# Splitting queries, keys and values where they are produced, loading heads one ahead, spacing the head norm, and moving attention traffic to GpSimd's DMA queue

## The chip, the cores and the metric

One core of a Trainium2 chip runs the whole program. The metric is device time in microseconds (us) of one execution; three executions of the kernel before gave a median of 3043.97 us.

## The reference: what is computed

One layer of a hybrid encoder, for a batch "s" of 1024 tokens and a batch "p" of 512 tokens, model width 2048, all in fp32:

```python
def mixer_layer(x, ...):
    h = rms_norm(x, norm_g) @ w_in
    qa, ka, va, ga, qb, kb, vb, gb = split(h)        # 5376 columns of features, 1280 of values
    oa = window_gqa(qa, ka, va, sink, rel_bias)      # A: 16 heads of 64, 4 key heads, keys within 128 tokens
    ob = diff_attention(qb, kb, vb, lam, ...)        # B: 8 heads, all keys
    mixed = concatenate([silu(ga) * oa, silu(gb) * ob])
    return x + mixed @ w_out                         # then rms_norm(., final_g)

def diff_attention(q, k, v, lam, ...):               # per head, block of 128 queries
    s = einsum(q, k) * scale + bias                  # two score maps, c = 0, 1
    p = softmax(s)
    pd = p[0] - lam * p[1]
    o = pd @ v
    return rms_norm(o, subln_g) * (1 - lam_init)     # over the head's 128 columns
```

## The kernel before: tiling, stages and order

Every fp32 product is made of three float32r products: an operand is split into hi (a cast on ACT) and lo = operand - hi (a subtraction on DVE), and hi·hi, lo·hi and hi·lo are summed in PSUM. Projections (L254 `project`, L291 `in_v`) take 16 slices of 128 features; the three matmuls of a slice are L263, L264, L266 (512 columns) or L301, L303, L305 (256 columns, for values). The weights' split stands just ahead of their use: `weights` (L242) loads a tile "wr", casts "wh" on ACT (L249) and subtracts "wl" on DVE (L251).

Stages. First `in_v_all` for s (values). Then `in_fm_all` for s (42 feature tiles of queries, keys, gates) beside attention A of s. Then a main line (values and features of p, the output projection of s in two chunks, that of p) beside a side line (attention B of s, A of p, B of p). `drive` (L654) interleaves the two: each step of the side line asks for a GAP of main's work (1.05 us a step in B of s, 1.3 in B of p, 2.1 and 1.7 in A). The order on each engine is fixed when the program is built, and every engine takes its instructions in that order; all transfers stand in one queue, SP's.

Features go to DRAM (`fm_s`, `fm_p`, from `in_fm`), values to `v_s`, `v_p` (`in_v`, L314, L315), and attention loads them back unsplit. Attention A (L369): `load_head` loads the keys twice (partitions 0-63 and 64-127), splits them (L366, L376), and `load_q` (L391, L392) loads four pieces for every block of 128 queries and splits them (L393, L394). Attention B (L492): `load_head` (L497) loads strip, keys and values and splits them on ACT (L366, L511) and DVE (L505, L512) when the head begins; `load_q` (L516) does so every four blocks (L521). For a block and each of the two maps, `scores` (L524) makes s (L535, L536), takes the minimum of -(s + bias) on DVE (L538), the exponential on ACT (L542), and after the second map 1/z (L546, L547), p1 scaled on ACT (L548) and p0·z0 - p1·z1 on DVE (L549). `turn` (L551) transposes the block before (L558, into the PSUM tile "tp", one buffer in s, two in p) and splits it into "ph" on ACT (L560) and "pl" on DVE (L561). `values` (L563) multiplies with the values (L572 to L574).

When a head's values are done, `normalise` (L580) is emitted six steps later, in one go: squares, ssq (L588), 1/rms "rc" by a square root on ACT (L183, a table load before and after it) and a reciprocal on DVE (L184); rc is stored to DRAM as single elements (L591, `rstd_s`, `rstd_p`), loaded back along rows on every partition as "r" (L595), the gate is loaded (L597), and DVE multiplies gate·output (L598) and ·r (L599); the product goes to `mix` (L600), from which `load_mix` brings it into the output projection.

Of the kernel before, what the change touches and what calls it, by code (L numbers as in the profile page):

```python
# [9 lines left out]
F32 = mybir.dt.float32  # L10
# [23 lines left out]
WR = [3]  # L34
# [11 lines left out]
def kernel(  # L46
# [23 lines left out]
    dma = nc.sync.dma_start  # L70

# [7 lines left out]
    ones_r = const.tile([P, P], F32R, name="ones_r")  # L79
    V.tensor_copy(ones_r, ones)  # L80
# [8 lines left out]
    lamv = const.tile([P, 2], F32, name="lamv")  # L89
    lsum = const.tile([P, 2], F32, name="lsum")  # L90

    def constants():
# [7 lines left out]
        nc.gpsimd.memset(lamv, 1.0)  # L100
# [11 lines left out]
        V.tensor_tensor(out=lamv[:, 1:2], in0=lsum[:, 0:1], in1=lsum[:, 1:2], op=ALU.subtract)  # L112
        V.tensor_scalar(out=lamv[:, 1:2], in0=lamv[:, 1:2], scalar1=LAM_INIT, scalar2=None, op0=ALU.add)
# [39 lines left out]
    def make_batch(nm, xt, yt, ntok, normed):  # L153
# [4 lines left out]
        b.fm = [dram.tile([P, ntok], F32, name=f"fm_{nm}{c}") for c in range(N_FM)]  # L158
        b.v = [dram.tile([ntok, 256], F32, name=f"v_{nm}{g}") for g in range(5)]
        b.rstd = [dram.tile([1, ntok], F32, name=f"rstd_{nm}{h}") for h in range(HB)]  # L160
# [25 lines left out]
    def rstd_cols(acc, psp):  # L186
        """1/rms of each token from its partial sums of squares, a column per 128 tokens."""
# [7 lines left out]
    def rstd_rows(rc, psp, pool=None, **kw):  # L195
        """The same along rows, on every partition: in PSUM, or copied to a tile of the pool."""
# [31 lines left out]
    def load_mix(b, c, pool):  # L228
        """Yields after each feature tile that it has brought in and split."""
        ch = new_chunk()  # L230
        yield ch
        for k in range(KT):
            hi = pool.tile([P, TC], F32R, name="hi")
            lo = pool.tile([P, TC], F32R, name="lo")
            dma(out=raw(lo), in_=b.mix[c][k])
# [6 lines left out]
    def weights(src, wp, before=None):  # L242
        a, c = src.shape[1], src.shape[2]
        wr = wp.tile([P, a, c], F32, name="wr", bufs=WR[0])
        dma(out=wr, in_=src)
        if before:
            before()
        wh = wp.tile([P, a, c], F32R, name="wh")
        S.copy(out=wh, in_=wr)  # L249
        wl = wp.tile([P, a, c], F32R, name="wl")  # L250
        V.tensor_tensor(out=wl, in0=wr, in1=raw(wh), op=ALU.subtract)  # L251
        return wh, wl

    def project(chs, w, psp, wp, along=iter(()), ahead=iter(())):  # L254
        ps = [psp.tile([P, 512], F32, name="pp") for _ in chs]
        for part in range(4):
            for _ in range(4):
                next(ahead, None)
            wh, wl = weights(w[:, 4 * part:4 * part + 4, :], wp)
# [12 lines left out]
    def in_fm(b, chs, c, psp, wp):  # L272
        ps = yield from project(chs, w_fm[c], psp, wp)
        gate = c >= C_GA
        f = 0.125 if c < C_KB or C_QA <= c < C_KA else 1.0
        for n, ch in enumerate(chs):
            o = ev.tile([P, TC], F32, name="o", bufs=2)
            h = ps[n]
            if not b.normed:
                V.scalar_tensor_tensor(out=o, in0=h, scalar=f, in1=b.rb[n], op0=ALU.mult, op1=ALU.mult)  # L280
                h = o
            elif not gate:
                S.activation(out=o, in_=h, func=AF.Copy, scale=f)
            if gate:
                th = ev.tile([P, TC], F32, name="sq", bufs=2)
                S.activation(out=th, in_=h, func=AF.Tanh, scale=0.5)
                V.scalar_tensor_tensor(out=o, in0=th, scalar=1.0, in1=h, op0=ALU.add, op1=ALU.mult)
            dma(out=b.fm[c][:, n * TC:(n + 1) * TC], in_=o)
        done.add((b.nm, "fm", c))

    def in_v(b, chs, g, psp, wp, before=None):  # L291
        ps = [[psp.tile([P, 2, 256], F32, name="pp") for _ in range(2)] for _ in chs]
        for part in range(8):
            wh, wl = weights(w_v[g][:, 2 * part:2 * part + 2, :], wp, before and (lambda: before(g, part)))
# [15 lines left out]
        for n, ch in enumerate(chs):  # L310
            for t in range(4):
                o = ev.tile([P, 256], F32, name="ov", bufs=2)
# [8 lines left out]

    def in_fm_all(b, chs, psp, wp):
        order = []
        for pr in range(2):
            order += [C_KA + pr] + [C_QA + 4 * pr + j for j in range(4)] + [C_GA + 4 * pr + j for j in range(4)]
        for h in range(HB):
            order += [C_KB + h, C_QB + h, C_GB + h]
        for c in order:
            yield from in_fm(b, chs, c, psp, wp)

    def out_proj(b, c, mix, psp, wp, yp, before):
        """Returns the steps left for when the next products are under way: norm and store."""
# [3 lines left out]
        for d in range(KT):  # L336
            xr = yp.tile([P, TC], F32, name="xr", bufs=2)
            dma(out=xr, in_=b.xt[d * P:(d + 1) * P, c * TC:(c + 1) * TC])
            ps = yield from project([ch], w_o[d], psp, wp, before, mix)
# [4 lines left out]
        def finish(spread):  # L344
# [3 lines left out]
            for d in range(KT):  # L348
                yield
                V.scalar_tensor_tensor(out=y[d], in0=y[d], scalar=fg[:, d:d + 1], in1=r, op0=ALU.mult, op1=ALU.mult)  # L350
                dma(out=b.yt[d * P:(d + 1) * P, c * TC:(c + 1) * TC], in_=y[d])
# [8 lines left out]
    def load_qk(at, tagname, src, n, bufs=2):  # L360
        """src [64, n] rows in DRAM -> raw copy on partitions 0-63 and 64-127, and its high part."""
        lo = at.tile([P, n], F32R, name=f"{tagname}_lo", bufs=bufs)
        dma(out=raw(lo)[0:DH], in_=src)
        dma(out=raw(lo)[DH:P], in_=src)
        hi = at.tile([P, n], F32R, name=f"{tagname}_hi", bufs=bufs)
        S.copy(out=hi, in_=raw(lo))  # L366
        return hi, lo

    def attention_a(b, at, gap, pss, pst, pso, psp):  # L369
        n, nb = b.n, b.nb  # L370

        def load_head(kv):
            lo_rows = slice(DH, P) if kv % 2 == 0 else slice(0, DH)
            rows = slice(0, DH) if kv % 2 == 0 else slice(DH, P)
            k_hi, k_lo = load_qk(at, "k", b.fm[C_KA + kv // 2][(kv % 2) * DH:(kv % 2 + 1) * DH, :], n, 1)
            V.tensor_tensor(out=k_lo, in0=raw(k_lo), in1=raw(k_hi), op=ALU.subtract)  # L376
            vv = at.tile([P, nb, P], F32R, name="vv")
# [460 lines left out]
```

## Time and profile before

| | us |
|---|---|
| median of 3 runs | 3043.97 (3041.66 to 3049.67) |
| profiled execution: span from first to last instruction | 3051.6 |
| TensorE busy in it | 2897.0 (95%) |
| DVE, ACT busy | 1635.5, 1336.9 |

The profile is of one more execution. What lay around its span is not listed, so its own time is at least the span, 7.6 us above the median. "Busy" for TensorE (PE) counts a matmul from its start to its modelled end, and at half clock a matmul is busy longer. PEclk is the granted clock as a share of 2.4 GHz.

### The profile page before, as it was taken

What the parts mean: (1) busy time and instruction counts of PE and PEld (TensorE: products, weight loads), DVE (VectorE), ACT (ScalarE), POOL (GpSimd) and SP (SyncE); (2) the same over time, 40 slices, a digit from 0 to 9 for tenths busy, and PEclk for the clock granted to TensorE, in tenths of its full rate; (3) what the DMA queues carried; (4) which work ended last, traced back from release to release, by engine and by line L of the source; (5) the groups of instructions that cost most, each with busy time, mean ns of one, the idle gap of its engine ahead of it and who ended that gap; (6) DMA issues with size and microseconds to landing.
All of it is one profiled execution on the core that took longest, in us unless ns stands there. A gap on an engine that the chain in (4) does not pass through costs nothing.

```text
span 3051.6 us, 41709 instructions
## 1 busy us (share of the span) xinstructions
PE 2897.0 (95%) x15178; PEld 2439.3 (80%) x15178; DVE 1635.5 (54%) x3335; ACT 1336.9 (44%) x2577; POOL 1.0 (0%) x10
## 2 busy tenths in 40 slices
PE   9999999999999999989989998999999997888997
PEld 8998888888888887879878777787788876667786
DVE  6111135565655553266566766675478776654634
ACT  6111123343434332155556565565456465453321
POOL 0000000000000000000000000000000000000000
PEclk9999999999999999999999999999999998999998
DMA  6622222232323232243343443433456456643633
GB/s 197 225 74 82 77 76 84 84 102 83 107 82 102 82 116 74 73 146 117 100 126 101 140 118 103 112 110 86 135 159 191 138 150 170 176 127 100 218 118 120
DMA packets 268250, 364.67 MB, mean 120 GB/s; under 512 B 50487, under 2 KB 123703, under 8 KB 267020
## 3 DMA queue, kind: packets, MB, share of 16 engines
q1 hardware_dynamic: 268044, 362.00, 39.4%
q8 instruction: 119, 1.95, 0.3%
q14 instruction: 87, 0.71, 0.1%
HBM read 295.67 MB, written 78.79 MB: 123 GB/s over the span
## 4 chain that ended last, share of the span: by engine, by line
PE 42%; DMA 11%; DVE 3%; ACT 3%; issue 2%; SPq 1%; DVEq 0%; ACTq 0%
PE pp L266 10%; PE pp L264 10%; PE pp L263 10%; DMA rstd_s<-rc 2%; DMA rstd_p<-rc 2%; PE tp L558 2%; PE s L535 2%; PE s L536 2%; DMA r<-rstd_p 1%; DMA r<-rstd_s 1%; PE o_ps L572 1%; PE o_ps L574 1%; PE o_ps L573 1%; PE pp L301 1%; PE pp L305 1%
## 5 line engine op out<-in xcount | busy, mean ns | idle before, releaser
L263 PE MATMUL pp<-hi,wh 128*128 128x512 f32 x2784 | 1132.4, 407 | 6.1 <-ACT wh L249 5.9
L264 PE MATMUL pp<-lo,wh 128*128 128x512 f32 x2784 | 1111.0, 399 | 0.0
L266 PE MATMUL pp<-hi,wl 128*128 128x512 f32 x2784 | 1002.2, 399 | 31.7 <-DVE wl L251 31.6
L251 DVE TENSOR_TENSOR wl<-wr,wh 128x512 fp32r<-128x512 f32 x608 | 417.2, 688 | 572.4 <-ACT wh L249 547.9
L249 ACT CAST wh<-wr 128x512 fp32r<-128x512 f32 x608 | 374.3, 617 | 788.4 <-PE pp L264 606.6
L266 PEld LDWEIGHTS pp<-hi,wl 128*128 128x128 f32 x2784 | 528.4, 190 | 163.6 <-DVE wl L251 38.8
L263 PEld LDWEIGHTS pp<-hi,wh 128*128 128x128 f32 x2784 | 529.5, 190 | 103.7 <-ACT wh L249 7.0
L264 PEld LDWEIGHTS pp<-lo,wh 128*128 128x128 f32 x2784 | 530.4, 191 | 100.3
L301 PE MATMUL pp<-wh,hi 128*128 128x256 f32 x960 | 275.0, 287 | 10.9 <-ACT hi L223 6.3
L303 PE MATMUL pp<-wl,hi 128*128 128x256 f32 x960 | 272.3, 284 | 4.3 <-DVE wl L251 4.3
L305 PE MATMUL pp<-wh,lo 128*128 128x256 f32 x960 | 272.1, 284 | 0.0
L542 ACT ACTIVATE t<-t,nm 128x1024 f32<-128x1024 f32 (+1 forms) x192 | 193.6, 1008 | 112.1 <-DVE nm L538 111.0
L538 DVE CUSTOM_DVE_ANT_0 t<-s,strip 128x1024 f32<-128x1024 f32 (+1 forms) x192 | 199.7, 1042 | 54.0 <-PE s L536 53.5
L301 PEld LDWEIGHTS pp<-wh,hi 128*128 128x128 f32 x960 | 183.4, 191 | 17.7 <-ACT wh L249 7.4
L303 PEld LDWEIGHTS pp<-wl,hi 128*128 128x128 f32 x960 | 184.0, 192 | 6.1 <-DVE wl L251 5.1
L305 PEld LDWEIGHTS pp<-wh,lo 128*128 128x128 f32 x960 | 182.8, 191 | 0.1
L558 PE MATMUL tp<-ident,t 128*128 128x128 f32 x640 | 102.9, 285 | 64.3 <-DVE t L549 50.4
L436 ACT CAST ph<-tp 128x512 fp32r<-128x512 f32 (+1 forms) x160 | 79.8, 502 | 166.7 <-PE tp L434 165.0
L417 ACT ACTIVATE t<-t,nm 128x384 f32<-128x384 f32 (+1 forms) x192 | 109.8, 573 | 96.6 <-DVE nm L413 95.7
L558 PEld LDWEIGHTS tp<-ident,t 128*128 128x128 f32 x640 | 80.7, 146 | 87.9 <-issue 40.2
L437 DVE TENSOR_TENSOR pl<-tp,ph 128x512 fp32r<-128x512 f32 (+1 forms) x160 | 92.8, 582 | 101.5 <-ACT ph L436 100.8
L561 DVE TENSOR_TENSOR pl<-tp,ph 128x512 fp32r<-128x512 f32 x160 | 110.3, 689 | 68.8 <-ACT ph L560 66.0
(111 smaller groups left out, 3113.0 us busy)
## 6 DMA issues: line engine op xcount, KB each, us to landing
wr<-in_w_fm_dram SPq DMA_DIRECT2D x336, 256.0 KB, 3.2
wr<-in_w_o_dram SPq DMA_DIRECT2D x192, 256.0 KB, 3.3
fm_s<-o SPq DMA_DIRECT2D x84, 256.0 KB, 2.1
wr<-in_w_v_dram SPq DMA_DIRECT2D x80, 256.0 KB, 2.9
xr<-in_xt_s_dram SPq DMA_DIRECT2D x64, 256.0 KB, 3.8
out_dram<-y SPq DMA_DIRECT2D x48, 256.0 KB, 3.8
fm_p<-o SPq DMA_DIRECT2D x42, 256.0 KB, 2.3
k_lo<-fm_s SPq DMA_DIRECT2D x40, 256.0 KB, 4.1
```

The source lines that it names most:

```text
L249: S.copy(out=wh, in_=wr)
L251: V.tensor_tensor(out=wl, in0=wr, in1=raw(wh), op=ALU.subtract)
L263: T.matmul(ps[n], lhsT=wh[:, j, :], rhs=ch.hi[k], start=(k == 0), stop=False)
L264: T.matmul(ps[n], lhsT=wh[:, j, :], rhs=ch.lo[k], start=False, stop=False)
L266: T.matmul(ps[n], lhsT=wl[:, j, :], rhs=ch.hi[k], start=False, stop=(k == KT - 1))
L301: T.matmul(o, lhsT=ch.hi[k][:, tok], rhs=wh[:, j, :], start=(k == 0 and t % 2 == 0), stop=False, skip_group_check=True)
L303: T.matmul(o, lhsT=ch.hi[k][:, tok], rhs=wl[:, j, :], start=False, stop=False, skip_group_check=True)
L305: T.matmul(o, lhsT=ch.lo[k][:, tok], rhs=wh[:, j, :], start=False, stop=(k == KT - 1), skip_group_check=True)
L538: V.tensor_tensor_reduce(out=t, in0=s, in1=u.head.strip[:, x0:x0 + n], scale=-1.0, scalar=3.0e38, op0=ALU.add, op1=ALU.min, accum_out=u.nm ...
L542: S.activation(out=t, in_=t, func=AF.Exp, scale=-1.0, bias=u.nm[:, m:m + 1], accum_out=u.z[:, m:m + 1])
L558: T.transpose(out=tp[:, j, :], in_=u.p[0][:, kk * P:(kk + 1) * P], identity=ident)
L561: V.tensor_tensor(out=pl[:, :, qi, :], in0=tp, in1=raw(ph)[:, :, qi, :], op=ALU.subtract)
```

## The change

- `in_fm` stores the feature tiles of queries and keys twice, hi in `fm` and lo in the new `fml`, and `in_v` stores values as `v` and `vl`; attention loads the halves, with no split of its own.
- A class `Weights` loads tiles three ahead and splits them two (stage 1 and 2) or three (stage 3) ahead.
- Attention B loads the next head at the second last block of this one, transposes a block two blocks behind the scores instead of one, and forms p0 - p1·(lam·z0/z1) in one DVE operation (L579); the missing 1/z0 is put right in the head norm, where eps is multiplied by z0². ACT's scaling of p1 and the square root with its table loads are gone; the power -0.5 is taken on GpSimd (L625).
- `normalise` is a generator: ssq and the store of rc, then four steps later the loads of r and gate ("nt", two buffers), four steps later the products (L636, L637) and the store, one step later the second chunk.
- `pdma` is `nc.gpsimd.dma_start`: all loads and stores of attention, the stores of features and values, the loads of `mix` and the stores of the output go to GpSimd's queue. Weights, x and constants stay on SP.

The diff, cut:

```diff
     def in_fm(b, chs, c, psp, wp):
...
             if gate:
...
-            dma(out=b.fm[c][:, n * TC:(n + 1) * TC], in_=o)
+                pdma(out=b.fm[c][:, sl], in_=o)
+                continue
+            if b.normed:
+                S.activation(out=hi, in_=h, func=AF.Copy, scale=f)
+                V.scalar_tensor_tensor(out=o, in0=h, scalar=f, in1=th, op0=ALU.mult, op1=ALU.subtract)
+            else:
+                S.copy(out=hi, in_=o)
+                V.tensor_tensor(out=o, in0=o, in1=th, op=ALU.subtract)
+            pdma(out=b.fm[c][:, sl], in_=th)
+            pdma(out=b.fml[c][:, sl], in_=o)
...
     def in_v(b, chs, g, psp, wp, before=None):
...
-                S.activation(out=o, in_=ps[n][t // 2][:, t % 2, :], func=AF.Copy, scale=f)
-                dma(out=b.v[g][n * TC + t * P:n * TC + (t + 1) * P, :], in_=o)
+                S.activation(out=o[:, 0, :].bitcast(F32R), in_=h, func=AF.Copy, scale=f)
+                V.scalar_tensor_tensor(out=o[:, 1, :], in0=h, scalar=f, in1=o[:, 0, :], op0=ALU.mult, op1=ALU.subtract)
+                tok = slice(n * TC + t * P, n * TC + (t + 1) * P)
+                pdma(out=b.v[g][tok, :], in_=o[:, 0, :])
+                pdma(out=b.vl[g][tok, :], in_=o[:, 1, :])
...
+    class Weights:
...
+        def split(self, n):
+            while len(self.ready) < n and (self.raw or self.todo):
+                self.load()
+                wr = self.raw.pop(0)
+                wh = self.wp.tile([P, 512], F32R, name="wh", bufs=self.splits)
+                S.copy(out=wh, in_=wr)
+                wl = self.wp.tile([P, 512], F32R, name="wl", bufs=self.splits)
+                V.tensor_tensor(out=wl, in0=wr, in1=raw(wh), op=ALU.subtract)
+                self.ready.append((wh, wl))
+                self.load()
...
     def attention_b(b, at, gap, pss, pst, pso, psp):
...
+        def load_q(hd, j):
+
+            qq = at.tile([P, 2, 2, 2 * P], F32R, name="qq", bufs=2)
+            for x, fm in enumerate((b.fm, b.fml)):
+                src = fm[C_QB + hd.h][:, j * 2 * P:(j + 1) * 2 * P].rearrange("(m d) t -> d m t", d=DH)
+                pdma(out=raw(qq)[0:DH, :, x, :], in_=src)
+                pdma(out=raw(qq)[DH:P, :, x, :], in_=src)
+            return qq
...
-                S.activation(out=p1, in_=p1, func=AF.Copy, scale=u.z[:, 1:2])
-                V.scalar_tensor_tensor(out=p0, in0=p0, scalar=u.z[:, 0:1], in1=p1, op0=ALU.mult, op1=ALU.subtract)
...
+                V.scalar_tensor_tensor(out=u.p, in0=t, scalar=u.z[:, 1:2], in1=u.p, op0=ALU.mult, op1=ALU.add)
...
         def normalise(hd):
...
-            ssq = psp.tile([P, 512], F32, name="pp")
+            ssq = pst.tile([P, 4, P], F32, name="tp")[:, 0, 0:nb]
...
-            rsqrt_mean(rc, ssq[:, 0:nb], P)
-            dma(out=b.rstd[h].rearrange("a (i p) -> p (a i)", p=P), in_=rc)
+            V.scalar_tensor_tensor(out=rc, in0=hd.z0, scalar=eps[:, 0:1], in1=hd.z0, op0=ALU.mult, op1=ALU.mult)
+            V.scalar_tensor_tensor(out=rc, in0=ssq, scalar=1.0 / P, in1=rc, op0=ALU.mult, op1=ALU.add)
+            nc.gpsimd.tensor_tensor(out=rc, in0=rc, in1=mhalf[:, 0:nb], op=ALU.pow)
+            pdma(out=b.rstd[h].rearrange("a (i p) -> p (a i)", p=P), in_=rc)
+            wait = 4
             for c in range(b.nch):
+                yield wait
...
-                dma(out=r, in_=b.rstd[h][:, sl].to_broadcast([P, TC]))
+                pdma(out=r, in_=b.rstd[h][:, sl].to_broadcast([P, TC]))
...
-                dma(out=gt, in_=b.fm[C_GB + h][:, sl])
+                pdma(out=gt, in_=b.fm[C_GB + h][:, sl])
+                yield 4
...
-                dma(out=b.mix[c][8 + h], in_=gt)
+                pdma(out=b.mix[c][8 + h], in_=gt)
+                wait = 1
...
+                if i == nb - 2 and h + 1 < HB and not any(k not in done for k in keys_of(h + 1)):
+                    ahead = load_head(h + 1)
                 u = Record()
...
+                steps = turns(behind.pop(0)) if len(behind) == 2 else iter(())
```

Where instructions stand. First DVE in attention B of s, around the norm of the sixth head. Before (L184 is 1/rms, "wl" the weights' split, "s,strip" the pass over scores, "pl" the split of a transposed piece, L599 the product with r):

```order
L184 RECIPROCAL rc<-rc 128x8
L251 TENSOR_TENSOR wl<-wr,wh 128x512
L521 TENSOR_TENSOR q_hi<-q_lo,q_hi 64x512
L538 ISA t,nm<-s,strip 128x1024
L538 ISA nm 128x1
L561 TENSOR_TENSOR pl<-tp,ph 128x4x128
L521 TENSOR_TENSOR q_hi<-q_lo,q_hi 64x512
L251 TENSOR_TENSOR wl<-wr,wh 128x512
L599 TENSOR_TENSOR gt<-gt,r 128x512
```

And with the change (L624 is the mean square, L579 the one combination, L636 and L637 the products with gate and r):

```order
L624 SCALAR_TENSOR_TENSOR rc<-tp,rc 128x8
L321 SCALAR_TENSOR_TENSOR o<-pp,sq 128x512
L264 TENSOR_TENSOR wl<-wr,wh 128x512
L577 RECIPROCAL z<-z 128x1
L578 SCALAR_TENSOR_TENSOR z<-z_17742,nlam,z 128x1
L579 SCALAR_TENSOR_TENSOR t_18256<-t_18280,z,t_18256 128x1024
L591 TENSOR_TENSOR pl<-tp,ph 128x4x128
L264 TENSOR_TENSOR wl<-wr,wh 128x512
L568 ISA t_18376,nm<-s,strip 128x1024
L568 ISA nm 128x1
L264 TENSOR_TENSOR wl<-wr,wh 128x512
L591 TENSOR_TENSOR pl<-tp,ph 128x4x128
L636 SCALAR_TENSOR_TENSOR nt<-nt,sg,osb 128x512
L637 TENSOR_TENSOR nt<-nt 128x512
```

Between 1/rms and the first product that needs the loads stood 7 rows, and now stand 11; both times rows of scores, transposes and weights are behind it on DVE. What feeds PE behind it is "pl", the pass over scores and "wl".

Second, the transfers around that norm. Before, on SP's queue:

```order
L591 DMA rstd_s_154<-rc 128x8x1
L245 DMA wr<-in_w_fm_dram 128x512
L363 DMA q_lo<-fm_s_109 64x512
L364 DMA q_lo<-fm_s_109 64x512
L595 DMA r<-rstd_s_154 128x512
L363 DMA q_lo<-fm_s_109 64x512
L245 DMA wr<-in_w_fm_dram 128x512
L600 DMA mix_s_13_170<-gt 128x512
L595 DMA r<-rstd_s_154 128x512
```

With the change, on GpSimd's queue (the norm of a head of s, with the power, the store of rc, and the loads "nt"):

```order
L625 TENSOR_TENSOR rc<-rc,mhalf 128x8
L552 DMA qq<-fml_s_147 64x2x256
L626 DMA rstd_s_182<-rc 128x8x1
L553 DMA qq<-fml_s_147 64x2x256
L632 DMA nt<-rstd_s_182 128x512
L634 DMA nt<-fm_s_138 128x512
L638 DMA mix_s_10_198<-nt 128x512
L632 DMA nt<-rstd_s_182 128x512
L317 DMA fm_p_248<-o 128x512
L634 DMA nt<-fm_s_138 128x512
L638 DMA mix_s_10_214<-nt 128x512
L552 DMA qq<-fm_s_106 64x2x256
```

The store, the loads and the queries stood among weights on SP; now they stand among queries, values and stores of features, and the weights' loads are in the other queue.

Third, an attention A block of p on GpSimd's queue with the change:

```order
L484 DMA gt<-fm_p_246 64x128
L484 DMA gt<-fm_p_247 64x128
L426 DMA qq<-fm_p_238 64x2x128
L427 DMA qq<-fm_p_238 64x2x128
L426 DMA qq<-fml_p_280 64x2x128
L427 DMA qq<-fml_p_280 64x2x128
L426 DMA qq<-fm_p_239 64x2x128
L427 DMA qq<-fm_p_239 64x2x128
L317 DMA fm_p_259<-o 128x512
L426 DMA qq<-fml_p_281 64x2x128
L427 DMA qq<-fml_p_281 64x2x128
L491 DMA mix_p_2_308<-oa 64x128
```

Eight loads of queries a block (four before), two gates and two stores for each pair of heads. Of the 1544 rows of GpSimd, 591 stand from the start to the end of attention A of s, and 311 in that of p; before it had 15 rows.

## Rows read from the trace of the kernel before

**Rows 1.** The page, busy time and instructions by engine.

```profile
PE 2897.0 (95%) x15178; PEld 2439.3 (80%) x15178; DVE 1635.5 (54%) x3335; ACT 1336.9 (44%) x2577; POOL 1.0 (0%) x10
```

**Rows 2.** Windows by stage: busy us (instructions) of each engine, PEclk, DMA share, GB/s.

```profile
450.00:1130.00 680.00, 679.97 (x3361) 564.98 (x3361) 390.85 (x1023) 261.66 (x651) 0.00 (x0) 1.00 0.30 89
...
1310.00:2160.00 850.00, 787.52 (x4468) 678.75 (x4467) 530.58 (x861) 498.22 (x791) 0.00 (x0) 0.96 0.40 114
2160.00:2430.00 270.00, 260.10 (x1293) 214.55 (x1292) 199.91 (x533) 149.56 (x369) 0.00 (x0) 0.98 0.54 161
2430.00:2850.00 420.00, 365.68 (x1678) 292.94 (x1677) 251.95 (x513) 225.26 (x424) 0.00 (x0) 0.93 0.54 154
```

**Rows 3.** Windows of 50 us in attention B of s, first and last pair.

```profile
1550.00:1600.00 50.00, 42.14 (x221) 35.52 (x220) 29.43 (x48) 28.21 (x44) 0.00 (x0) 0.93 0.39 117
1600.00:1650.00 50.00, 50.00 (x262) 41.73 (x261) 36.07 (x59) 33.60 (x53) 0.00 (x0) 1.00 0.42 123
2050.00:2100.00 50.00, 43.68 (x222) 36.17 (x221) 28.48 (x47) 26.96 (x43) 0.00 (x0) 0.93 0.34 90
2100.00:2150.00 50.00, 50.00 (x270) 42.17 (x269) 25.24 (x42) 25.91 (x42) 0.00 (x0) 1.00 0.25 78
```

**Rows 4.** Windows full of 512-column and 256-column matmuls (PE alone).

```profile
250.00:300.00 50.00, 50.00 (x216) 1.00 0.28 88
100.00:200.00 100.00, 100.00 (x847) 1.00 0.45 152
```

**Rows 5.** Lines on PE in 2430:2850: busy, mean ns | idle before.

```profile
L263 PE MATMUL pp<-hi,wh 128*128 128x512 f32 x383 | 159.4, 416 | 6.1 <-ACT wh L249 5.9
...
L558 PE MATMUL tp<-ident,t 128*128 128x128 f32 x128 | 22.0, 300 | 21.9 <-DVE t L549 21.9
L572 PE MATMUL o_ps<-ph,v_hi 128*128 128x256 f32 x64 | 18.2, 285 | 0.3 <-ACT ph L560 0.3
```

**Rows 6.** Timeline of one head's norm in s: start, us, engine, line [idle <-releaser].

```profile
1965.26 0.20 DVE L184 RECIPROCAL rc<-rc 128x8 f32<-128x8 f32 x1
...
1965.48 0.38 SPq L591 DMA_DIRECT2D rstd_s<-rc  x1
...
1976.97 0.33 SPq L595 DMA_DIRECT2D r<-rstd_s  x1
...
1982.63 0.69 DVE L599 TENSOR_TENSOR gt<-gt,r 128x512 f32<-128x512 f32 x1 [11.09 <-DMA r<-rstd_s]
...
1986.76 1.09 PE L558 MATMUL tp<-ident,t 128*128 128x128 f32 x4 [10.14 <-DVE t L549]
```

**Rows 7.** Waits in 1310:2160: total, times, longest.

```profile
DVE gt L599 <- DMA r<-rstd_s: 63.3, 7, 11.1
```

**Rows 8.** Waits in 2430:2850: total, times, longest.

```profile
DVE gt L599 <- DMA r<-rstd_p: 45.2, 8, 10.9
```

**Rows 9.** DMA issues: count, KB each, median us to landing.

```profile
v_s<-ov SPq DMA_DIRECT2D x40, 128.0 KB, 3.3
...
r<-rstd_s SPq DMA_DIRECT2D x16, 256.0 KB, 4.9
...
q_lo<-fm_p SPq DMA_DIRECT2D x64, 64.0 KB, 3.0
...
rstd_s<-rc SPq DMA_DIRECT2D x8, 4.0 KB, 10.3
rstd_p<-rc SPq DMA_DIRECT2D x8, 2.0 KB, 9.3
```

**Rows 10.** Timeline of SP's queue in attention A of p: time to issue.

```profile
2202.61 1.24 SPq L452 DMA_DIRECT2D gt<-fm_p  x2
...
2207.74 0.60 SPq L391 DMA_DIRECT2D q_lo<-fm_p  x1
```

**Rows 11.** Lines over the span: busy, mean ns | idle before.

```profile
L548 ACT ACTIVATE t<-t,z 128x1024 f32<-128x1024 f32 (+1 forms) x96 | 96.7, 1008 | 77.5 <-DVE z L547 77.1
...
L424 DVE TENSOR_SCALAR t<-t,z 128x384 f32<-128x384 f32 (+1 forms) x192 | 67.3, 392 | 2.3
```

More of the change, by code (lines that the diff above doesn't have):

```diff
@@ L33 @@
 LATE = 4
-WR = [3]
 GAP_AS = 2.1
@@ L240, in load_mix, with __init__, load, next @@
             yield
[L242 to L254, printed above, removed]
+    class Weights:
+        def __init__(self, wp, order, loads, splits):
+            self.wp, self.todo, self.loads, self.splits = wp, order, loads, splits
+            self.raw, self.ready = [], []
+        def load(self):
+            while self.todo and len(self.raw) < self.loads:
+                wr = self.wp.tile([P, 512], F32, name="wr", bufs=self.loads)
+                src = self.todo.pop(0)
+                dma(out=wr.rearrange("p (a c) -> p a c", a=src.shape[1]), in_=src)
+                self.raw.append(wr)
+        def split(self, n):
[8 more added lines that the diff above has]
+                self.load()
+        def next(self, a, before=None):
+            self.load()
+            if before:
+                before()
+            self.split(self.splits)
+            wh, wl = self.ready.pop(0)
+            return tuple(t.rearrange("p (a c) -> p a c", a=a) for t in (wh, wl))
+    def tiles_v():
+        return [w_v[g][:, 2 * part:2 * part + 2, :] for g in range(5) for part in range(8)]
+    def tiles_p(w, cs):
+        return [w[c][:, 4 * part:4 * part + 4, :] for c in cs for part in range(4)]
+    def project(chs, psp, wp, along=iter(()), ahead=iter(())):
         ps = [psp.tile([P, 512], F32, name="pp") for _ in chs]
@@ L258, in project @@
                 next(ahead, None)
-            wh, wl = weights(w[:, 4 * part:4 * part + 4, :], wp)
+            wh, wl = wp.next(4)
             for j in range(4):
@@ L293, in in_v @@
         for part in range(8):
-            wh, wl = weights(w_v[g][:, 2 * part:2 * part + 2, :], wp, before and (lambda: before(g, part)))
+            wh, wl = wp.next(2, before and (lambda: before(g, part)))
             for j in range(2):
@@ L625, in attention_b @@
                     yield slot()
-                    if prev and m < nq:
-                        turn(prev, m)
+                    for _ in steps:
                         yield slot()
-                if prev and prev.i % 2 == 1:
-                    ready += [(prev.pair, part) for part in range(4)]
+                        break
+                for _ in steps:
+                    yield slot()
                 for _ in range(2):
@@ L634, in attention_b @@
                         yield slot()
-                prev = u
-        for m in range(nq):
-            turn(prev, m)
-            yield slot()
-        ready += [(prev.pair, part) for part in range(4)]
+                behind.append(u)
+        for u in behind:
+            for _ in turns(u):
+                yield slot()
         for x in ready:
@@ L733 @@
                 split_x(ch_p, raws[k], k, act)
-    WR[0] = 4
-    with w_pool("wp2", 3) as wp, ps_pool("psp2", 2, "left") as psp:
+    with w_pool("wp2", 3) as wp2, ps_pool("psp2", 2, "left") as psp:
+        wp = Weights(wp2, tiles_v() + tiles_p(w_fm, order_fm) + 3 * tiles_p(w_o, range(KT)), 3, 3)
         def main():
```

194 lines of the change are left out of this document (98 added, 96 removed).

## The prediction

> **What bounds the kernel now.** I read the page's busy times first: PE is busy 2897.0 us of a span of 3051.6, DVE 1635.5, ACT 1336.9 [rows 1]. So PE is the bound on average, and an edit can only save time where PE stands still or runs slowly. The change leaves the number of PE's products as it is. Next the windows by stage [rows 2]: in attention A of s PE is busy 679.97 of 680 us at full clock, so nothing is to be had there; in A of p 260.10 of 270; in attention B of s 787.52 of 850 at a mean clock of 0.96, and in B of p 365.68 of 420 at 0.93. The time to be had lies in B, about twice 80 us as follows.
>
> B of s, by windows of 50 us [rows 3]. They alternate: a full one (262 to 270 instructions on PE at clock 1.00) and one with a head's norm (204 to 222 at 0.90 to 0.93). Over the six pairs from 1550 to 2150 the means are 265.2 and 215.5, so a head loses (265.2 - 215.5) / 265.2 x 50 = 9.4 us, and eight heads 75 us.
>
> B of p has no undisturbed stretch, so I count its products and price them by full windows [rows 4]: 50 / 216 = 0.2315 us for 512 columns, 100 / 847 = 0.118 for 256. In 2430 to 2850 stand 3 x 383.3 products of the projection, 128 of scores (from the program: 8 heads, 4 blocks, 2 maps, 2 products), 3 x 64 with values and 128 transposes [rows 5]. At most 0.118 for a transpose gives 1278 x 0.2315 + 320 x 0.118 = 333.6; 64 one-column products of the norm, taken at 0.1, make it 340. Lost: 420 - 340 = 80 us, 10 a head.
>
> What ends these stops is seen in one head's timeline [rows 6]. DVE has 1/rms at 1965.46; its store is issued at 1965.48 and the load of r that needs it only at 1976.97; DVE has stood 11.09 us in front of L599 when r lands (1982.63 - 11.09 = 1971.54). Everything behind it on DVE waits too, and PE stands 10.14 us for a transpose whose input is behind it. The waits in B give 63.3 us in 7 heads of s [rows 7] and 45.2 in 8 of p [rows 8]. The chain is a store of 10.3 us (9.3 in p) and a load of 4.9 [rows 9].
>
> **The change part by part, against the profiled span of 3051.6 us.** That is 7.6 above the median of the runs, so I take 7.6 off at the end.
>
> *Head norm and distance.* The chain remains: rc, store, load, product. In s it was 1982.63 - 1965.46 = 17.2 us. The power on GpSimd is added; it is not in the trace, from 0.2 us (the reciprocal of the same tile [rows 6]) to 1.2 (ACT's pass over 1024 columns is 1008 ns [rows 11]); I take 0.5, nearest to the small tile. In the new order DVE has 9 to 12 rows between rc and L636 where there were 8. With some 60 rows in a full window of 50 us [rows 3] a row is 0.83 us: DVE arrives 7.5 to 10 us after rc and still waits 17.7 - 10 = 8 to 10 us. The spacing by itself saves little. What changes is how long PE runs while DVE stands: transposes take a map two blocks old, and weights are split two tiles further on. In s there is one "tp" buffer, whose "pl" stands behind the waiting product, so PE can go on until its next transposes. A head has 16 of these; (94.4 us from head to head - 9.4) / 16 = 5.3 us. So 9 - 5.3, and a remainder for the clock, about 5 us a head stay: 75 - 40 = **35 saved** in s (bounds: 0, if PE is stopped at once; 75, if all is covered). In p there are two "tp" buffers and 4 turns a head, over 10 us apart, three score buffers, and keys are there before the head begins (ACT's split of them stood in the way before). I take 3 us a head as left, for the load of the next weights behind the wait: 80 - 24 = **56 saved** (bounds 0 and 80).
>
> *Splits at production.* The pass of ACT over p1 (96.7 us [rows 11]) and the splits in attention go, and two splits per feature tile and value piece come. Neither engine is the bound: DVE is at 530.58 of 850 us in B of s [rows 2]. Priced at nothing beside PE; where the norm's stop is short, it shortens DVE's catching up, which is in the 5 us above. At the evictions of p's values (two PSUM tiles, both in use) an extra DVE pass and a second store come onto PE's path; a store lands in 3.3 us or less [rows 9], beside one that was there. I take 0.6 us in each of 5 groups: **+3** (0 to +8).
>
> *The tail.* p's last norm begins later by 9 emitted steps, some 10 us of main's work less to cover its chain of 17 us, and the output projection of p needs it: **+5** (0 to +10).
>
> *Starts of stages.* Loading ahead doesn't reach the first head of a stage; priced at nothing (0 to -10).
>
> *The queues.* SP loses all but weights and x, so weights no longer wait behind stores of attention. GpSimd gets the rest: 591 rows up to the end of A of s, which lasts 680 us, and 311 in A of p, which lasts 270. Before, GpSimd issued no transfer, so the price c of one is not in the trace. From below: SP's own time for the same transfers, 0.60 for a piece of q and 1.24 / 2 = 0.62 for a gate [rows 10]. From above: that one is only issued when the one before has landed, 3.0 us for q [rows 9]. A of p is paced by the queue from 270 / 311 = 0.87 us, A of s from 680 / 591 = 1.15. I take 0.6, since issuing and landing are separate rows and SP has several under way: 187 of 270 us and 355 of 680, both beside PE: **0**. By the upper end: 311 x 3.0 - 270 + 591 x 3.0 - 680 = +1756, which nothing in the trace comes near.
>
> The Trainium skill, DMA: Bandwidth & Descriptors, section Specifications, gives about 1 us to the first byte for a transfer of GpSimd and 0.6 for one of SP; taken as an estimate of c, 1.0 would add 311 - 270 = 41 us and make the sum 3002. Its section Issuing engine by pattern prefers SP for simple loads and stores; no run here yet shows either.
>
> Sum: 3051.6 - 35 - 56 + 3 + 5 = 2968.6; less 7.6, **2961 us**, 83 below the median.
>
> **The rivals.**
>
> *The stop only moves.* For it: the chain of 17 us and DVE's place in it are nearly as before, and the new loads stand behind queries and stores in GpSimd's queue, where a late one delays all. Against it: maps two blocks old. Then s gains nothing and p a third (27): 3044 - 27 + 8 = 3025, or 3044 if the queue adds 2 us a head more.
>
> *GpSimd's queue paces A of p.* With c between 0.87 and 1.1 the sum grows by up to 311 x 1.1 - 270 = 72: 2961 to 3033. For it: the same transfers took 0.6 of each slot on SP, and 8 pieces of q a block take the place of 4. Against it: nothing measured.
>
> *GpSimd's queue paces both A stages: slower.* The place is the loads of qq ahead of the scores; the price at c = 1.2 is 311 x 1.2 - 270 = 103 and 591 x 1.2 - 680 = 29, so 2961 + 132 = 3093. It turns the sign from 311c - 270 = 83, c = 1.13 us. For it: every transfer of attention in one queue that must also wait, row by row, for stores to land. Against it: c would be twice SP's. A variant has the same sign: DVE's scaling L424, 67.3 us in both A stages [rows 11], holding up GpSimd while it lasts, adds at most those 67.3 us to the queue's time.
>
> The Trainium skill, SBUF — State Buffer, section Who interferes with whom, says that operations of L424's kind can take a port that GpSimd needs to write its descriptors; no run here shows it yet, and at c = 0.6 the queue would still be under A of p's time (at most 187 + 67 of 270).
>
> **How the numbers follow.** The forecast has 0.50 (its own range 2925 to 3000, from the bounds of s and p taken half way); the stop that moves 0.16, half of it within 0.3% of 3044 (3035 to 3053, about what a measurement of this kernel can tell from no change); the queue in A of p 0.14; the queue in both 0.20. So faster 0.50 + 0.08 + 0.14 = 0.72, same 0.08, slower 0.20. Below 2890 (all of 155 saved) I leave 0.06, above 3080 0.14: 2890 to 3080.
>
> **What would show it.** Right: windows of B with a norm at 240 instructions or more on PE; DVE's wait for r still 8 to 10 us a head while PE's idle before the transposes is under 6; A of s still 680 us at full PE; GpSimd's issue of a piece of q at 0.6 to 0.8 us. Wrong: A of p longer than 280 us, or A of s with PE idle in front of scores whose queries have not landed (c over the thresholds above); the wait of PE for transposes still near 10 us a head (the stop only moved); no wait on r at all (I missed how far the steps are spaced, and 2900 is near).

## The result, and the profile after

The changed kernel took 3085.11 us (median of 4 runs, 3079.34 to 3088.63) against 3044.56 for the one before: a ratio of 1.0127, 95% interval 1.0112 to 1.0142. It is slower by 1.3%, where 83 us less were forecast. Its profiled span is 3077.6 us, 26.0 more than before. The medians lie 40.6 apart: the profile before is of a long execution (span 7.0 us above its median), the one after of the shortest of four (5.8 below). So the traces account for 26 of the 40.6 us, and the rest lies in the scatter between executions, which no trace here shows.

The page's busy times, the answer to [rows 1]:

```profile
PE 2898.2 (94%) x15178; PEld 2449.6 (80%) x15178; DVE 1600.4 (52%) x3328; ACT 1143.5 (37%) x2329; POOL 951.4 (31%) x1638
```

PE has the same work. ACT is freed of 193 us and DVE of 35, which does not show in the time; GpSimd is busy 951 us, nearly all of it issuing transfers. The windows by stage, the answer to [rows 2]:

```profile
450.00:1130.00 680.00, 680.00 (x3360) 566.80 (x3359) 379.19 (x1003) 255.89 (x641) 334.02 (x589) 1.00 0.39 114
...
1310.00:2160.00 850.00, 783.64 (x4449) 675.94 (x4448) 512.12 (x862) 371.17 (x655) 198.43 (x318) 0.96 0.48 137
2160.00:2430.00 270.00, 252.87 (x1238) 208.88 (x1237) 174.41 (x469) 127.84 (x316) 182.16 (x315) 0.96 0.65 180
2430.00:2850.00 420.00, 376.38 (x1743) 304.88 (x1741) 231.85 (x506) 166.86 (x341) 118.87 (x193) 0.93 0.60 159
```

Attention A of s is full as before. B of p and B of s (fixed windows, while stages begin 17 to 38 us later now) still run at clocks of 0.93 and 0.96, as before: the stops that were to be shortened are there.

To see where the 26 us came from I cut the span at the same points of the program (first product of the features, first and last scores of each attention, last product of squares) and priced the PE instructions recorded in each piece by the full windows of [rows 4]: 0.2315 us for 512 columns and 0.118 for 256; 0.175 for 384, 0.106 for a transpose and 0.1 for one column are estimates between and beside them, the same for all kernels. What a piece lasts longer than that is **lost** PE time. One profile each, so a few us are noise. The columns to the right are experiments told below.

| lost, us | before | after | E2 | E3 | E4 | E5 | E10 |
|---|---|---|---|---|---|---|---|
| values of s | 14.5 | 30.1 | 27.9 | 14.6 | 13.9 | 18.4 | 12.9 |
| features and A of s, rest | 22.9 | 21.8 | 19.3 | 23.6 | 16.8 | 21.4 | 21.1 |
| B of s | 83.6 | 88.1 | 27.8 | 16.4 | 80.8 | 89.4 | 18.3 |
| from B of s to A of p | 8.7 | 17.7 | 18.0 | 8.4 | 12.6 | 12.1 | 17.0 |
| A of p | 11.1 | 10.6 | 9.3 | 11.1 | 27.9 | 8.5 | 8.7 |
| B of p | 71.0 | 66.7 | 24.4 | 67.3 | 62.7 | 79.2 | 26.6 |
| tail | 28.7 | 31.4 | 36.3 | 28.2 | 33.1 | 28.5 | 34.9 |
| sum | 240.5 | 266.4 | 163.0 | 169.6 | 247.8 | 257.5 | 139.5 |

So three pieces made the result: the values of s (+15.6), the way to A of p (+9.0), and B, which was to give back 91 us and gave 0 (+4.5 and -4.3).

**B.** One head's norm in the timeline after, the answer to [rows 6]; columns are start, length, engine, line, and in brackets the idle time before and its releaser:

```profile
1679.82 0.17 DVE L624 SCALAR_TENSOR_TENSOR rc<-tp,rc 128x8 f32<-128x8 f32 x1 [0.45 <-PE tp L621]
...
1680.07 1.66 POOL L625 TENSOR_TENSOR rc<-rc,mhalf 128x8 f32<-128x8 f32 x1 [0.46 <-DVE rc L624]
...
1682.33 0.91 POOL L626 DMA_DIRECT2D rstd_s<-rc  x1
...
1691.97 0.60 POOL L632 DMA_DIRECT2D nt<-rstd_s  x1 [8.14 <-DMA rstd_s<-rc]
1692.56 0.55 POOL L634 DMA_DIRECT2D nt<-fm_s  x1
1697.27 0.75 DVE L636 SCALAR_TENSOR_TENSOR nt<-nt,sg,osb 128x512 f32<-128x512 f32 x1 [9.14 <-DMA nt<-fm_s]
...
1699.40 1.11 PE L588 MATMUL tp<-ident,t 128*128 128x128 f32 x4 [7.70 <-DVE pl L591]
```

DVE has the mean square at 1679.99. The power takes GpSimd 1.66 us, the store is issued 2.3 us after the mean square, the load of r when the store has landed at 1691.97, and the gate's load only behind it, since both are in one queue. DVE, which came to L636 at 1688.13, starts it at 1697.27: a chain of 17.3 us, as before (17.2), and a wait of 9.1 us. PE runs on until 1691.70, 3.6 us, and resumes 2.1 us after DVE does, when L637 and "pl" are done: a stop of 7.7 us. The waits of DVE for the norm, the answer to [rows 7, 8] (total, times, longest):

```profile
DVE nt L636 <- DMA nt<-fm_s: 91.3, 14, 11.3
...
DVE nt L636 <- DMA nt<-fm_p: 66.4, 7, 13.3
```

These are the waits of all eight heads and, in s, of both 512-token chunks of a head; [rows 7] has seven of the first chunks alone. Over the whole span before, the first chunk of s waited at L599 and the second at L598, for its gate:

```profile
DVE gt L599 <- DMA r<-rstd_s: 71.1, 8, 11.1
...
DVE gt L598 <- DMA gt<-fm_s: 20.2, 8, 6.9
```

So in s DVE waits 91.3 us in all, before and after: the first chunks went from 71.1 to 75.6 (8.9 to 9.5 a head), the second from 20.2 to 15.7. In p it waits 66.4 where it waited 45.2. PE's waits for transposes in B of s, from behind the first head's norm to the last scores, after and then before:

```profile
PE tp L588 <- DVE pl L591: 48.8, 8, 8.4
```

```profile
PE tp L558 <- DVE t L549: 28.5, 5, 10.1
PE tp L558 <- DVE pl L561: 10.4, 4, 7.9
```

Before, nine stops made 38.9 us; now eight make 48.8. The windows from the first to the last scores of B of s, after and then before, show what such a stop costs beside the standing:

```profile
1352.10:2134.00 781.90, 718.31 (x4099) 619.81 (x4098) 479.03 (x811) 343.69 (x609) 186.24 (x298) 0.96 0.48 139
```

```profile
1334.00:2121.40 787.40, 731.62 (x4169) 631.26 (x4170) 505.47 (x824) 472.44 (x751) 0.00 (x0) 0.96 0.39 114
```

PE stands 63.6 us after and 55.8 before. The rest of the 88.1 and 83.6 lost, 24.5 and 27.8 us or some 3 a head, is products that took longer, at a granted clock of 0.96 in both: in the head above the 512-column products took 0.39 us ahead of the stop and 0.63 and 0.77 right behind it. In B of p PE's waits after are these:

```profile
PE pp L295 <- DVE wl L264: 16.3, 4, 7.8
PE o_ps L603 <- DVE pl L591: 10.5, 7, 7.0
PE o_ps L602 <- ACT ph L590: 8.4, 3, 4.2
```

There PE stands at the weights' split and at the two halves of transposed pieces. The split and one half are DVE's work; the other half is cast on ACT, in whose queue weights' casts and exponentials stand that wait on DVE in their turn.

**The values of s.** ACT's evictions of the last value tiles wait for the second store of an earlier one:

```profile
256.72 0.47 ACT L353 ACTIVATE ov<-pp,rc 128x256 fp32r<-128x256 f32 x1 [2.61 <-DMA vl_s<-ov]
...
261.42 0.47 ACT L353 ACTIVATE ov<-pp,rc 128x256 fp32r<-128x256 f32 x1 [0.79 <-DMA vl_s<-ov]
```

and the first product of the features waits for the last of them (waits of PE in 100:450):

```profile
PE pp L292 <- DVE ov L354: 9.7, 1, 9.7
```

That wait is 9.7 of the 15.6 us. A store of values was issued in 0.54 us on GpSimd and in 0.32 on SP when all went back there (E4, below); minimum, median and maximum in ns:

```profile
L356 POOL DMA_DIRECT2D v_s<-ov x40: 540/540/683, 60.2 to 262.2; - x40
```

```profile
L356 SPq DMA_DIRECT2D v_s<-ov x40: 319/320/538, 58.8 to 252.7; - x40
```

From issue to landing its median was 2.1 us on GpSimd and 1.8 on SP. With two stores a tile and two buffers this price stands in the chain of the evictions.

**The way to A of p.** The last products of B's norm, their store, the first load and the first scores of A:

```profile
2192.43 0.68 DVE L637 TENSOR_TENSOR nt<-nt 128x512 f32<-128x512 f32 x1
...
2193.41 0.54 POOL L638 DMA_DIRECT2D mix_s<-nt  x1 [5.20 <-DVE nt L637]
...
2193.95 0.53 POOL L414 DMA_DIRECT2D kk<-fm_p  x1
...
2207.68 0.77 PE L444 MATMUL s<-kk,qq 128*128 128x256 f32 x2 [7.35 <-DMA qq<-fml_p]
```

A of p's loads begin 1.5 us after the last head's last product L637 starts, and the scores 13.7 us after the first load. The same before:

```profile
2146.49 0.20 DVE L184 RECIPROCAL rc<-rc 128x8 f32<-128x8 f32 x1 [3.38 <-ACT rc L183]
...
2170.67 0.69 DVE L599 TENSOR_TENSOR gt<-gt,r 128x512 f32<-128x512 f32 x1
...
2172.38 0.45 SPq L363 DMA_DIRECT2D k_lo<-fm_p  x1
...
2182.89 0.38 PE L411 MATMUL s<-k_hi,q_hi 128*128 128x256 f32 x1
```

From 1/rms to the last product it was 24.0 us and is 29.9 (from the mean square, at 2162.54); from the first load to the scores it was 10.5 and is 13.7.

### The profile page after: what moved, and what is told of

It is laid out like the page before. It is cut to its first block, busy times and chain, and to the rows that moved or that the text cites. A ratio compares the mean times of both kernels' runs of the same rounds, so it can differ in the third digit from the quotient of the medians.

```text
span 3077.6 us, 42232 instructions
## 1 busy us (share of the span) xinstructions
PE 2898.2 (94%) x15178; PEld 2449.6 (80%) x15178; DVE 1600.4 (52%) x3328; ACT 1143.5 (37%) x2329; POOL 951.4 (31%) x1638
## 3 DMA queue, kind: packets, MB, share of 16 engines
q0 software_dynamic: 82880, 225.60, 25.3%
## 5 line engine op out<-in xcount | busy, mean ns | idle before, releaser
L339 PE MATMUL pp<-wh,hi 128*128 128x256 f32 x960 | 275.7, 287 | 16.8 <-ACT hi L224 9.0
L566 PE MATMUL s<-kk,qq 128*128 128x512 f32 x640 | 183.8, 400 | 5.0 <-DVE nm L568 5.0
```

The costliest lines, as they stand in the source:

```text
L339: T.matmul(o, lhsT=ch.hi[k][:, tok], rhs=wh[:, j, :], start=(k == 0 and t % 2 == 0), stop=False, skip_group_check=True)
L566: T.matmul(s[:, sl], lhsT=u.q[:, m, x, tok], rhs=u.head.kk[:, m, sl], start=(x == 0), stop=(x == 1))
```

## The experiments

The ratio stands to the kernel before, run on the same chip.

**E1: more steps** in `normalise` of the changed kernel:

```diff
-            wait = 4
+            wait = 12
...
-                yield 4
+                yield 8
```

> The changed kernel with its head norm spaced further as written: 12 steps instead of 4 ahead of the loads, 8 instead of 4 ahead of the products. Theory 1 (the place of the product on DVE is set by the scheduler that orders the program, some 9 to 12 rows behind rc whatever number of steps is written, and the chain of 17 us is longer than those rows): nothing moves, 3085 us within 10, DVE still waits for the loads of the norm some 155 us in all. Rival (the steps act as written, 4 were too few): the waits go, B loses some 70 us less, about 3015.

3073.27 us, ratio 1.0100 (1.0078 to 1.0122), 2 us under the range expected; its interval meets that of the change. In s the first L636 of a head is the 9th to 12th row of DVE behind rc in seven heads and the 5th in the last, the same as without the edit; in p it is the 5th to 14th in seven heads and the 60th in one, where it was the 5th to 24th. DVE's waits are 91.7 and 71.2 us. So written steps moved the product far back in one head of sixteen. That the scheduler which orders the program puts an operation where by its own reckoning its data are there is my reading; no run shows how it decides.

**E2: a dependence in place of steps.** On the changed kernel:

```diff
-                yield 4
-                V.scalar_tensor_tensor(out=gt, in0=gt, scalar=sg[:, 0:1], ...)
+                yield 6
+                late = at.tile([P, 1], F32, name="late", bufs=2)
+                V.tensor_scalar(out=late, in0=newest[0], scalar1=0.0, scalar2=sg[:, 0:1], op0=ALU.mult, op1=ALU.add)
+                V.scalar_tensor_tensor(out=gt, in0=gt, scalar=late[:, 0:1], ...)
```

`newest[0]` is the weight z of the block whose scores were made last; the first wait is 6 steps instead of 4.

> The changed kernel with the norm's product made to depend on the newest block's weight z (its scalar becomes sg + 0*z of a block emitted 12 steps after rc, one operation on a 128x1 tile more per chunk), so that it can't be placed on DVE ahead of that block; in the built order it stands 22 to 31 rows behind rc instead of 9 to 12. Theory 1 (the stop of PE in B is DVE's early arrival at the product): DVE's waits for the norm fall from 158 us to under 40, the time lost by PE in attention B of s from 69 to about 25 us and of p from 67 to about 30; about 3005 us (2985 to 3025). Rival (PE's stops in B come from late queries and keys in GpSimd's queue or from the split of weights): DVE's wait goes, PE stops for something else, above 3060.

2977.12 us, ratio 0.9781 (0.9762 to 0.9801), 8 us under the range expected. DVE's waits for the norm fell to 34.9 us, and B of s, by the fixed window, to PE busy 817 of 850 at a clock of 0.98:

```profile
DVE nt L639 <- DMA nt<-fm_p: 17.6, 2, 9.4
DVE nt L639 <- DMA nt<-fm_s: 17.3, 2, 10.9
```

```profile
1310.00:2160.00 850.00, 817.13 (x4654) 703.56 (x4654) 534.70 (x939) 387.20 (x696) 230.09 (x371) 0.98 0.53 149
```

Lost time in B of s fell from 88 to 28 us and in B of p from 67 to 24. With E1 beside it, which has more steps and no dependence, the cause of PE's stops in B is shown: it is DVE's early place in front of the norm's loads.

**E3: the same dependence on the kernel before**, and nothing else of the change:

```diff
+            wait = 11
...
+                yield wait
+                wait = 5
+                late = at.tile([P, 1], F32, name="late", bufs=2)
+                V.tensor_scalar(out=late, in0=newest[0], scalar1=0.0, scalar2=sg[:, 0:1], op0=ALU.mult, op1=ALU.add)
-                V.scalar_tensor_tensor(out=gt, in0=gt, scalar=sg[:, 0:1], ...)
+                V.scalar_tensor_tensor(out=gt, in0=gt, scalar=late[:, 0:1], ...)
```

> The kernel before with only this: loads of r and gate at once as before, the products 11 and 5 steps later and made to depend on the newest block's z in the same way (in the built order 18 to 40 rows behind rc instead of 8). No other part of the change. Theory 1: the 10 us a head that PE lost go, less a rest for the second chunk (one buffer for r and gate, so its loads wait for the first product): about 2960 us (2935 to 2985). Rival 2 (it needs the transposes two blocks behind and the weights split ahead, since PE stops at the next wait on DVE in any case): above 3015.

2981.04 us, ratio 0.9791 (0.9770 to 0.9813): faster by some 2%, inside the range and short of the 2960. B of s went from 84 to 16 us lost, without transposes further behind or weights split further ahead; B of p stayed at 67. Waits of ACT there:

```profile
ACT k_hi L366 <- DMA k_lo<-fm_p: 56.5, 12, 7.5
```

**E4: all transfers back on SP** in the changed kernel:

```diff
-    pdma = nc.gpsimd.dma_start
+    pdma = nc.sync.dma_start
```

> The changed kernel with every transfer that it moved to GpSimd's queue back on SP's queue. Theory 3 (GpSimd's queue costs by its order, not by its price: first loads of attention A of p stand behind the last norm's stores, and the value stores land late): the start of A of p loses 9 us less and the values of s up to 10 less, but the loads of weights now stand behind the norm's load that waits 10 us for its store: 3065 to 3085. Rival (the second queue is what keeps weights on time): 3105 or more, with PE waiting for weights in B.

3058.37 us, ratio 1.0048 (1.0029 to 1.0067): 27 us better than the change and 7 under the range expected, so the rival fell. The values of s lose 13.9 us, so it is their stores in GpSimd's queue that cost, not the second DVE pass. A of p loses 27.9: SP must now issue eight pieces of q a block among weights, and 11.3 us of this are PE's waits for them:

```profile
PE s L444 <- DMA qq<-fm_p: 7.1, 7, 2.9
...
PE s L444 <- DMA qq<-fml_p: 4.2, 4, 2.2
```

**E5: only the values' stores and the norm's transfers on SP**, in the changed kernel; all six lines as the first:

```diff
-                pdma(out=b.v[g][tok, :], in_=o[:, 0, :])
+                dma(out=b.v[g][tok, :], in_=o[:, 0, :])
```

> The changed kernel with two groups of transfers back on SP's queue: the stores of values, and the head norm's store, loads and result. Theory 3 (GpSimd's queue costs 27 us by its order, in two places): the values of s lose 14 us instead of 30, the way from B of s to A of p 9 to 12 instead of 18, and A of p stays at 11, since its pieces of q stay on GpSimd; B is unchanged: about 3060 us (3050 to 3070). Rival (the second pass and store of the values cost by themselves, whatever the queue): values of s still lose 25 or more, 3075 or above.

3069.52 us, ratio 1.0080 (1.0057 to 1.0103). The values gained 12 us and the way to A of p 6, so the rival fell; but B of p, expected unchanged, lost 12 more. SP's queue in B of p:

```profile
2610.13 0.38 SPq L626 DMA_DIRECT2D rstd_p<-rc  x1
2610.60 0.46 SPq L254 DMA_DIRECT2D wr<-in_w_o_dram  x1
2620.12 0.33 SPq L632 DMA_DIRECT2D nt<-rstd_p  x1
```

Between the store of rc and the load of r that waits for it (2610.13 to 2620.12) one tile of weights is issued. PE's wait for the weights' split in B of p is 33.9 us (16.3 in the change):

```profile
PE pp L295 <- DVE wl L264: 33.9, 5, 9.8
```

But DVE, which makes that split, also stands longer in front of the norm (88.9 us in p, 66.4 in the change), and ACT waits for weights 16.1 us there (7.7 in the change). With the same transfers on SP in E4 DVE's waits were 67.7 us and B of p lost 62.7. So these runs don't show that weights late on SP made the 12 us; why the norm took longer here stays open.

**E6: E2 and E5 together.**

> Both together: the products that depend on the newest block's z, and the values' stores and the norm's transfers on SP. If the two causes are apart, their gains add: 2977 - 20 to 25 = about 2955 us (2945 to 2965). Rival (the norm's load that waits for its store holds up the weights behind it on SP): PE waits for weights in B, 2975 or more.

2983.78 us, ratio 0.9808 (0.9789 to 0.9828): no better than E2, as the rival had it, and, as far as the trace tells, by its mechanism, one queue further on: B of p lost 52 us instead of 24, and PE's waits there are for the halves of transposed pieces (24.0 us). ACT, which casts one half, waits for weights 56.6 us meanwhile (22.8 in E2), and SP's queue stands 62.9 us in front of loads of r:

```profile
ACT wh L262 <- DMA wr<-in_w_o_dram: 56.6, 14, 8.8
```

```profile
SPq L633 <- DMA rstd_p<-rc: 62.9, 7, 10.1
```

**E7, E8: parts of the change taken out of E2.** First E7, then E8:

```diff
-                if i == nb - 2 and h + 1 < HB and not any(k not in done for k in keys_of(h + 1)):
-                    ahead = load_head(h + 1)
...
-                steps = turns(behind.pop(0)) if len(behind) == 2 else iter(())
+                steps = turns(behind.pop(0)) if len(behind) == 1 else iter(())
```

> The kernel with dependent products (2977 us) without loading the next head ahead: a head is loaded when its first block begins, as before the change. In the kernel before with dependent products B of p still lost 67 us where this one loses 24. Theory 4 (that is the loads at a head's start): B of p loses some 60 us again, B of s less than 30, about 3020 us (3005 to 3040). Rival (it is the transposes two blocks behind): within 10 us of 2977.

> The kernel with dependent products (2977 us), transposes one block behind the scores instead of two. Theory 4: within 10 us of 2977, since with DVE no longer standing there is no stop to cover. Rival (the lag is what carries B of p): B of p loses 50 us or more, 3005 or above.

E7: 2977.91 us (0.9784, 0.9763 to 0.9804), no difference: theory 4 fell. E8: 2966.06 us (0.9745, 0.9722 to 0.9769), 11 us better, with B of p at 20.9 and B of s at 18: with dependent products the second block of distance costs time instead of covering any.

**E9: E3 with only the norm's transfers on GpSimd's queue**, four lines as this:

```diff
-                dma(out=r, in_=b.rstd[h][:, sl].to_broadcast([P, TC]))
+                nc.gpsimd.dma_start(out=r, in_=b.rstd[h][:, sl].to_broadcast([P, TC]))
```

> The kernel before with dependent products (2981 us), and only the norm's transfers (store of rc, loads of r and gate, result) on GpSimd's queue. Theory 5 (in B of p the norm's load of r waits in its queue for its store, and what stands behind it is late: weights, keys, queries on SP): B of p loses 35 to 50 us instead of 67, about 2958 us (2945 to 2970). Rival (it is the split of keys and queries at a head's start, which the change moved to where they are produced): within 8 us of 2981.

2974.98 us, ratio 0.9772 (0.9754 to 0.9791). B of p lost 51.3 us instead of 67.3, and the tail 34.3 instead of 28.2. The 6 us gained are less than theory 5 asked and within the 8 that its rival allowed, so the norm's place in SP's queue is part of what B of p still loses and not all of it: ACT's waits for keys there went from 56.5 us to 42.7.

**E10, E11: the version that beats both.** E10 is the change with dependent products, transposes one block behind, and the values' stores on SP; E11 also loads the first key head of A on SP:

```diff
-                pdma(out=bias[:, g, :], in_=toeplitz(rep_a[kv * GRP + g], LA, 127, 384))
+                (pdma if kv else dma)(out=bias[:, g, :], in_=toeplitz(rep_a[kv * GRP + g], LA, 127, 384))
```

and so for its keys, values and first two blocks of q.

> The changed kernel with dependent products and transposes one block behind (2966 us), and only the stores of values on SP, the norm's transfers left on GpSimd's queue. Theory 3 for the values alone: values of s lose 15 to 18 us instead of 32, B of p stays near 21: about 2951 us (2943 to 2960). Rival (what B of p lost with both groups on SP came from the values of p): 2965 or more.

> The same with the loads of the first key head of attention A (keys, values, bias, and q of its first two blocks) on SP's queue as well, so that they don't stand behind the norm of the last head of B in GpSimd's queue. Theory 3: the way from B of s to A of p loses 9 to 12 us instead of 17, about 2944 us (2935 to 2955). Rival (A of p starts late for another reason, the drain of the last blocks of B): no change against the kernel above.

E10: 2953.13 us, ratio 0.9700 (0.9684 to 0.9715), the fastest; PE is busy 97% of its span:

```profile
PE 2862.2 (97%) x15178; PEld 2426.5 (82%) x15178; DVE 1603.6 (54%) x3352; ACT 1143.1 (39%) x2329; POOL 885.5 (30%) x1518
```

E11: 2958.82 us (0.9717, 0.9702 to 0.9732): the way to A of p still lost 16.5 us. In its timeline the last product of B's norm, the first load of A on SP and the first scores are these:

```profile
2101.40 0.68 DVE L640 TENSOR_TENSOR nt<-nt 128x512 f32<-128x512 f32 x1
...
2103.22 0.48 SPq L414 DMA_DIRECT2D kk<-fm_p  x1
...
2118.03 0.77 PE L444 MATMUL s<-kk,qq 128*128 128x256 f32 x2 [8.03 <-DMA qq<-fm_p]
```

The load follows the norm's last product there too, in another queue. `attention` opens A's SBUF pool when B's generator has ended, norm and all; that the loads wait for the room is argued from this and the code, and not tried by itself. The kernel before shows the same order (2170.67 and 2172.38).

**E12: E10 with weights split when asked for:**

```diff
-            self.split(self.splits)
+            self.split(1)
```

> The fastest kernel so far (dependent products, transposes one block behind, values' stores on SP: 2953 us), with each tile of weights split only when it is asked for instead of three tiles ahead. In B of p this kernel loses 27 us, the kernel before with dependent products and the norm's transfers on GpSimd's queue 51. Theory 6 (the rest is the loads and splits of keys and queries at a head's start, which the change moved): B of p stays under 35 us, about 2957 us (2948 to 2966). Rival (it is the weights split ahead): B of p loses 45 us or more, 2970 or above.

2956.26 us, ratio 0.9702 (0.9686 to 0.9719): no difference from E10, B of p at 32.0. With E7, E8 and E12 none of loading ahead, the lag and the split ahead carries B of p by itself. What makes B of p lose 67 us in E3 and 24 in E2 stays open. The keys and queries split at production are the likeliest, since ACT waited 56.5 us for their loads in E3. But the one combination in place of ACT's pass over p1, the norm without ACT's table loads, the other loads of attention on GpSimd's queue and weights loaded three ahead are also in E2 and not in E3, and no run has any of these alone.

## Why the prediction was wrong, step by step

- *Where the time is* held: A full, some 75 and 80 us in B. E2 gave back most of both, E3 that of s.
- *Head norm and distance* failed, in one step: that PE would go on 5.3 us in s, and so long in p that 3 us a head stay, while DVE stands, and that this was new. DVE's wait came as said (8 to 11 us a head in s, 6 to 13 in seven heads of p). But PE ran on only 3.6 us in the head shown and lost 2.1 more in resuming behind the products; and it had run on before too, which I had not taken off: 5.1 us in the head of [rows 6] (from 1971.54 to 1986.76 - 10.14), and 38.9 us of stops in nine places where DVE waited 8 to 11 us a head. That head, with 10.14 us, had the longest stop of them. The clock's share, some 3 us a head, I had at 1.3 (the 5 us left, less 9 - 5.3). In p two "tp" buffers were no cover, as weights and "pl" stand on the same engine behind the same wait. Saved 91, got 0. Small beside this: the spacing of 5.3 rests on 94.4 us from head to head, and the rows of L599 give 98.5, so 5.6.
- *The power*: 1.66 us on 128x8 elements (s) and 1.03 on 128x4 (p), against the 0.5 taken and a bound of 1.2. With it and the gate behind r the chain took 17.3 us in the head shown, near the 17.7 of the forecast.
- *The spacing*: "9 to 12 rows" was right and its cause not seen; the steps of the new generator have next to no effect on DVE's order (E1).
- *Splits at production*: no price on ACT and DVE shows, as said; PE's waits at the evictions of p's values are 1.6 us and were 1.3, for +3. The evictions of s were not priced at all: +15.6. With two buffers, two stores in GpSimd's queue and the features' first product behind the last eviction they were on PE's path.
- *Starts of stages* at nothing: +9.0. The last norm's chain grew by 5.9 us and A of p's first loads by 3.2, and the mean square itself came 28.5 us behind the last scores where 1/rms came 25.3. That the second chunk follows the first by 10 us is not new (9.5 before). With the norm's transfers on SP (E5) 6 us came back; the rest is not tried apart.
- *The tail*, +5: +2.7, right.
- *The queue's price*, c = 0.6: right for what it was read from, a piece of q (0.60 us on GpSimd too), and GpSimd was busy 334 of 680 us in A of s:

```profile
L426 POOL DMA_DIRECT2D qq<-fm_s x64: 592/604/729, 314.5 to 1085.9; - x64
```

Both A stages lost no more than before, so neither queue rival came, nor the variant with DVE's scaling: no issue of these 64 took over 0.73 us. The price does not hold for every transfer: a store of values takes 0.54 us against 0.32 on SP, the store of rc 0.92 against 0.38. So the queue cost by what stood in it and, at the values of s, by its price. The Trainium skill, DMA: Bandwidth & Descriptors, section Specifications, speaks of about 1 us to the first byte for a transfer of GpSimd; as a price of issuing, which I weighed it as, it did not hold here: 0.60 for a piece of q.

- *The rivals*: "the stop only moves" was the mechanism, with 0.16; its time of 3025 to 3044 lacked the 25 us of values and stage start and counted on a third of p's loss, of which 4 us came. The rival on the slower side was nearest in time, and its mechanism wrong.

## What to carry to other kernels

When an engine waits in front of a long chain, look first at where the order of the program puts the waiting instruction: steps in the source were no distance here, where a scheduler may move the operation; a data dependence was one, and one operation on 128x1 a chunk, with the products written later, was worth some 62 us on the kernel before. A second DMA queue is still in order, and its price must be read for each shape of transfer: here GpSimd's was SP's for pieces of q and 1.7 times SP's for plain tiles. What waits (a load for its store) should not share a queue with what feeds the busiest engine, and stores that free a small pair of buffers belong in the quicker queue. Measure how far the starved engine already runs on before counting a new cover.

## What the runs showed that I had not expected

GpSimd issues a piece of q as fast as SP (0.60 us), but a plain 128x512 tile in 0.54 us against 0.33, and the store of single elements (128x8) in 0.92 against 0.38; that store lands 9 to 10 us after its issue on either (medians). A power on 128x8 elements takes GpSimd 1.66 us. Moving transposes from two blocks behind to one was worth 11 us once DVE no longer stood.
